# An encoder layer on one core: the embedding gate from eight block products to seven, with its weight sums made during the mixers

## The chip, the core and the metric

The kernel runs on one core of a Trainium2 chip. A core has five engines that work side by side, each through its own list of instructions in order: TensorE (PE, matrix products into the PSUM banks), VectorE (DVE), ScalarE (ACT), GpSimd (POOL) and SyncE (SP), which here issues most of the DMAs. An instruction waits for semaphores of what it needs, and everything behind it on the same engine waits too. The metric is the device time of one execution in microseconds. Of the kernel before, three runs were timed; one further execution was recorded by the hardware profiler.

## The reference

One post-norm encoder layer on 1024 tokens of width 1024, in float32:

```python
u      = x @ W_in                       # 4 x 512 retention, 512 + 128 + 128 attention
group R: bidirectional retention, 8 heads, chunks of 128
group A: windowed attention, 8 query heads on 2 key heads, window 128, sink logit, ALiBi
mix    = concat(R, A) @ W_out
h      = LN1(alpha * x + mix)
ffn    = (silu(h @ W_gate) * (h @ W_up)) @ W_down          # hidden width 2816
ple    = sigmoid(h @ W_pg) * (p @ W_pe)                    # the embedding gate, 1024 x 1024
out    = LN2(alpha * h + ffn + ple)
```

The change concerns `ple`, above all its product `h @ W_pg`, and two places in the mixers.

## The kernel before

Each float32 product is made of three passes: an operand x is split into hi (ScalarE's copy, rounded) and lo = x − hi (VectorE's subtraction; `split`, L77 to L79), and TensorE adds hi·hi, hi·lo and lo·hi in one PSUM bank (`mm3` L81 to L84, and `mm3c` L274 to L278 where several products go into one bank). So a block product of four k tiles by four token tiles is 48 matmuls of 128x512.

The program runs in this order. First the projections `x @ W_in`, 0 to 165 us, with results kept or spilled to DRAM (`ud`). Then the mixers, four pairs i = 0 to 3 (165 to 405 us): each step list (L747 to L760) mixes turns, score products, softmax and values of the retention and the attention, and at every `F` some matmuls of further projections are taken from a queue (`take`, L419), so that TensorE has work between. Only TensorE's order is written out there; a scheduler places the other four engines' instructions. A *turn* is a transpose on TensorE into a PSUM bank, followed by a copy or a split. PSUM has eight banks, two of each of the tags mm, s, t and o; in the mixers, the projections use mm, and turns and the retention's `kv` use t. In pair 0, `first_keys` (L404) and `conv_q` (L385) build the split queries and keys, by ScalarE copies and VectorE operations on 64 partitions x 1024 elements. GpSimd makes the decay tables `sq` and `dt` (L498, L499), which `pt` (L549) needs, and small copies into `sc` (L625) for the scores.

W_out and the first norm follow (405 to 499 us); `to_hT` (L824) turns a token tile of h and splits it into the four blocks `HB[i, j]` (i: half of the features, j: half of the tokens), and scales the tile for the residual.

The embedding gate (499 to 595 us) is four calls of `ple` (L895): output half h by token half, eight k tiles each, 8 x 4 x 3 = 96 matmuls. Its weights come through `load_pg` (L889). Behind each call ScalarE takes the sigmoid (L912), GpSimd multiplies with the embedding piece `ed` (L913; `p @ W_pe` was made in the mixers) and VectorE adds to the residual tile (L914). Beside the calls, as `side`, go the last four `to_hT` and the token sums `t_sums`, from which the FFN's products take their operands. The residual tiles are then stored to `zd` in DRAM (L973, L976) and read back near the end (`load_acc`, L1195).

The FFN (from 595 us) makes gate and up by a scheme of seven block products in place of eight: token halves and feature halves give 2 x 2 blocks, sums of token blocks (TT) meet sums of weight blocks (`s_sums`, on GpSimd), and the seven products are combined. `ahead` (L1376) issues loads and splits a few units ahead. From the first FFN unit on (L1404) all five engines stand in program order.

Of the kernel before, what the change touches and what calls it, by code (L numbers as in the profile page):

```python
# [40 lines left out]
def layer(tc, xT, xn, w_first, w_mt, w_out, w_pg, w_pe, pT, w_gu, w_dn,  # L41
# [343 lines left out]
    def conv_q(i, raw):  # L385

        qs = [bt([P, S], "aq", 3, F32R) for _ in range(2)]
        for g in range(2):
# [4 lines left out]
            dve.scalar_tensor_tensor(qs[g][z, :], raw[a, :], sc_, qs[g][a, :].bitcast(F32), ALU.mult, ALU.subtract)
        return qs
# [7 lines left out]
    def first_keys():  # L402
        pairs[0][2] = conv_q(0, first[0])
        for g in range(2):  # L404
            a = slice(64 * g, 64 * g + 64)
            z = slice(64 * (1 - g), 64 * (1 - g) + 64)
            act.activation(k1[g][a, :], first[1][a, :], AF.Copy)
            dve.tensor_tensor(kz[g][a, :], first[1][a, :], k1[g][a, :].bitcast(F32), ALU.subtract)
            act.activation(k1[g][z, :], first[1][a, :], AF.Copy)
# [72 lines left out]
    class Retention:  # L482
# [1034 lines left out]
```

## Time and profile before

| | |
|---|---|
| median of 3 runs | 1240.6 us (1239.94 to 1241.23) |
| profiled execution | 1243.8 us, span of its trace 1242.0 us, mean granted TensorE clock 0.991 |
| mixers, 165 to 400 us | TensorE busy 218.04 of 235 |
| first gate matmul / first FFN matmul | 499.12 us / 595.42 us |
| TensorE busy, 530 to 610 us | 72.18 of 80 |
| instructions on PE, DVE, ACT, POOL in the trace | 5947, 1320, 922, 395 |

How to read the rows of the profile shown below. A timeline row has start and duration in us, engine, line of the kernel, operation, out<-in by the program's names, and in brackets the idle time of that engine just before and what ended it. A row of grouped instructions has count, then busy us and mean ns of one, then idle time before and its releasers. A row of waits reads "engine, line waited for: us in total, times, longest". A row by windows gives busy time and count of each engine, then the clock that TensorE was granted, the busy share of the DMA engines and GB/s. A row of DMA issues gives count, size and the median us from issue to landing.

### The profile page before, as it was taken

The page shows a single profiled execution, that of the slowest core. Times are in us where ns is not written, and L with a number is a line of the kernel's source. Part 1 is how long each engine was busy: PE and PEld are TensorE (multiplying, and loading weights), DVE is VectorE, ACT ScalarE, POOL GpSimd, SP SyncE. Part 2 cuts the span into 40 slices and gives each one's busy share as a digit, 9 for nine tenths or more (in the row PEclk, how much of TensorE's full clock was granted, in tenths as well). Part 3 has the DMA queues.
Part 4 walks back from the last instruction along what each step waited for, and adds up shares of the span by engine and source line. Part 5 has one row for each costly group of instructions (what it writes and reads, how often), then busy time and mean ns, then how long its engine had stood idle before and what let it go on. Part 6 is the DMA issues. An engine that isn't in the chain of part 4 may idle for free.

```text
span 1242.0 us, 16636 instructions
## 1 busy us (share of the span) xinstructions
PE 1203.1 (97%) x5947; PEld 993.0 (80%) x5947; DVE 772.5 (62%) x1320; ACT 496.9 (40%) x922; POOL 447.7 (36%) x395
## 2 busy tenths in 40 slices
PE   9999989999999999999899999999999999999996
PEld 7778868787878888878688888888888888888885
DVE  7954467777675658497455454555445555865667
ACT  5432355565656503433333233333323334553452
POOL 2652011112111011132467466465564523024235
PEclk9999989999999999999999999999999999999998
DMA  5223230242311422124422233312333149999977
GB/s 221 90 102 119 101 121 18 94 130 85 110 61 42 155 75 81 55 67 165 175 81 90 85 127 128 118 72 74 119 128 127 68 138 284 387 272 205 256 179 203
DMA packets 64899, 161.67 MB, mean 130 GB/s; under 512 B 7729, under 2 KB 9905, under 8 KB 64817
## 3 DMA queue, kind: packets, MB, share of 16 engines
q1 hardware_dynamic: 56176, 143.83, 32.9%
q0 software_dynamic: 8640, 16.78, 7.8%
q8 instruction: 47, 0.77, 0.2%
q14 instruction: 36, 0.29, 0.1%
HBM read 115.76 MB, written 39.58 MB: 125 GB/s over the span
## 4 chain that ended last, share of the span: by engine, by line
PE 66%; issue 9%; DMA 9%; DVE 8%; POOL 5%; ACT 2%; DVEq 0%; SPq 0%; POOLq 0%; ACTq 0%
PE bs L278 4%; PE bs L276 4%; PE bs L277 4%; PE bt L277 4%; PE bt L278 4%; PE bt L276 4%; PE bmm L276 3%; PE bmm L277 3%; PE bmm L278 3%; PE bo L276 3%; PE bo L277 3%; PE bo L278 3%; PE bmm L82 3%; PE bmm L83 3%; PE bmm L84 3%
## 5 line engine op out<-in xcount | busy, mean ns | idle before, releaser
L1035 POOL TENSOR_TENSOR ev<-ev 128x512 f32<-128x512 f32 x33 | 55.7, 1687 | 94.0 <-DVE ev L1050 64.5
L79 DVE TENSOR_TENSOR w<-raw,w 128x512 fp32r<-128x512 f32 x69 | 56.1, 824 | 45.6 <-ACT w L78 45.5
L79 DVE TENSOR_TENSOR w<-H,w 128x512 fp32r<-128x512 f32 x44 | 38.2, 868 | 62.0 <-ACT w L78 62.0
L625 POOL COPY sc<-skb 128x1 f32<-128x1 f32 x64 | 16.7, 269 | 154.5 <-PE bt L646 113.8
L1005 POOL TENSOR_TENSOR H<-ln 128x512 f32<-128x512 f32 x22 | 29.3, 1333 | 96.8 <-DMA ln<-in_w_gu 96.8
L1039 POOL TENSOR_TENSOR ev<-ev,ev 128x512 f32<-128x512 f32 x44 | 62.0, 1421 | 2.6
L1033 ACT ACTIVATE ev<-ev 128x512 f32<-128x512 f32 x33 | 20.9, 633 | 104.4 <-DVE ev L1050 104.4
L78 ACT ACTIVATE w<-raw 128x512 fp32r<-128x512 f32 x69 | 42.0, 625 | 47.9 <-DMA raw<-in_w_pg 13.6
L79 DVE TENSOR_TENSOR u<-H,u 128x512 fp32r<-128x512 f32 x47 | 35.4, 753 | 38.7 <-ACT u L78 38.4
L82 PE MATMUL bmm<-H,w 128*128 128x512 f32 x112 | 50.1, 448 | 0.2 <-ACT H L78 0.2
L913 POOL TENSOR_TENSOR sg<-sg,pe 128x512 f32<-128x512 f32 x16 | 25.1, 1585 | 59.0 <-ACT sg L912 55.5
L810 POOL TENSOR_TENSOR stt<-stt,cst 128x1 f32<-128x1 f32 x8 | 11.5, 1449 | 96.1 <-DVE stt L809 96.1
L78 ACT ACTIVATE u<-H 128x512 fp32r<-128x512 f32 x47 | 29.7, 631 | 40.6 <-PE bs L278 10.7
L634 ACT ACTIVATE sc<-sc,st 128x385 f32<-128x385 f32 (+1 forms) x64 | 37.1, 583 | 19.8 <-DVE st L632 19.6
L84 PE MATMUL bmm<-H,w 128*128 128x512 f32 x112 | 44.7, 399 | 0.0
L83 PE MATMUL bmm<-H,w 128*128 128x512 f32 x112 | 44.5, 397 | 0.0
L630 DVE CUSTOM_DVE_ANT_0 sc<-cst,bs,skb 128x384 f32<-128x384 f32 (+1 forms) x64 | 35.0, 574 | 8.1 <-PE bs L629 7.8
L1009 POOL TENSOR_TENSOR H<-raw,H 128x512 f32<-128x512 f32 x22 | 36.9, 1677 | 0.0
L78 ACT ACTIVATE w<-H 128x512 fp32r<-128x512 f32 x44 | 27.4, 623 | 23.0 <-PE bs L278 8.3
L648 ACT ACTIVATE ptr<-bt 128x384 f32<-128x384 f32 (+1 forms) x64 | 26.6, 457 | 24.7 <-PE bt L646 24.5
L79 DVE TENSOR_TENSOR u<-raw,u 128x512 fp32r<-128x512 f32 x30 | 33.4, 1112 | 5.0 <-ACT u L78 5.0
L914 DVE TENSOR_TENSOR acc<-acc,sg 128x512 f32<-128x512 f32 x16 | 19.1, 1219 | 27.3 <-POOL sg L913 27.3
(757 smaller groups left out, 4068.6 us busy)
## 6 DMA issues: line engine op xcount, KB each, us to landing
ad<-ev SPq DMA_DIRECT2D x33, 512.0 KB, 2.9
raw<-in_w_gu SPq DMA_DIRECT2D x22, 512.0 KB, 4.4
ln<-in_w_gu SPq DMA_DIRECT2D x22, 512.0 KB, 3.5
raw<-ad SPq DMA_DIRECT2D x40, 256.0 KB, 5.5
ln<-ad SPq DMA_DIRECT2D x37, 256.0 KB, 6.5
H<-in_w_dn SPq DMA_DIRECT2D x33, 256.0 KB, 7.1
raw<-in_w_mt SPq DMA_DIRECT2D x12, 512.0 KB, 3.6
h0b<-in_w_dn POOLq DMA_DIRECT2D x24, 256.0 KB, 7.3
```

Of the source, the lines that this page charges most:

```text
L78: act.activation(hi, raw, AF.Copy)
L79: dve.tensor_tensor(lo, raw, hi.bitcast(F32), ALU.subtract)
L82: pe.matmul(o, lh, rh, start=start, stop=False)
L83: pe.matmul(o, lh, rl, start=False, stop=False)
L84: pe.matmul(o, ll, rh, start=False, stop=stop)
L276: pe.matmul(o, lh, rh, start=start, stop=False, skip_group_check=True)
L277: pe.matmul(o, lh, rl, start=False, stop=False, skip_group_check=True)
L278: pe.matmul(o, ll, rh, start=False, stop=stop, skip_group_check=True)
L634: act.activation(sc[g][:, :nk + 1], sc[g][:, :nk + 1], AF.Exp, bias=st_[:, 1, j, g:g + 1], accum_out=st_[:, 2, j, g:g + 1])
L1009: pool.tensor_tensor(s[3], a(0, 1), s[0], ALU.subtract)
L1035: pool.tensor_tensor(c[:, 1, :], c[:, 0, :], c[:, 1, :], ALU.mult)
L1039: pool.tensor_tensor(self.ev[dst][:, 0, :], left, right, op)
```

## The change

1. **The embedding gate by seven products.** `h @ W_pg` is now computed by the same scheme as the FFN, on the same token sums: products 3, 7, 1, 6, 2, 5, 4, of 4 k tiles x 4 token tiles x 3 passes = 48 matmuls each, 336 in place of 384. The weight sums for products 5, 7, 6 and 3 (`ws`) are read from DRAM. The lo half of every second weight tile goes to GpSimd. Products 1 and 6 stay in their banks for products 2 and 5, and the results are combined on VectorE (u, v, f), with sigmoids on ScalarE. The multiplication with `ed` (`embed`, `embed_next`) is taken in single pieces: four on GpSimd, twelve on VectorE, of these eight between FFN units; a GpSimd DMA adds each result to `zd` in DRAM. `to_hT` therefore stores its scaled tile to `zd` at once. All four turns beside product 7 use the banks mm and s. The two token halves exchange their places (`tile_of`). All of it stands in program order on all five engines.
2. **Weight sums in the mixers.** `weight_sums`, twice in pair 0 and twice in pair 1, loads four blocks of W_pg, makes four sums on GpSimd and stores them: 16 loads, 16 sums of 128x512 and 16 stores in all.
3. **First keys in halves.** The operations of `conv_q` and `first_keys` run over 512 columns at a time, all of the first half first.
4. **Three banks for turns.** `tbank` gives the mixers' turns and `kv` the tags t, t, mm in rotation.

```diff
+    wsd = {p: dr.tile([2, P, D], F32, name=f"ws{p}") for p in (5, 6, 7, 3)}
...
     def first_keys():
         pairs[0][2] = conv_q(0, first[0])
-        for g in range(2):
...
+        for c in hs:
+            for g in range(2):
...
+                act.activation(k1[g][a, c], first[1][a, c], AF.Copy)
+                dve.tensor_tensor(kz[g][a, c], first[1][a, c], k1[g][a, c].bitcast(F32), ALU.subtract)
+                act.activation(k1[g][z, c], first[1][a, c], AF.Copy)
+
+    def weight_sums(kt):
+        a, b = atile((P, 2, HF)), atile((P, 2, HF))
+        q, c = kt // 2, hs[kt % 2]
+        for t, i in ((b, 1), (a, 0)):
+            for h in range(2):
+                sp.dma_start(t[:, h, :], w_pg[h, 2 * i + q][:, c])
+        a00, a10, a01, a11 = a[:, 0, :], a[:, 1, :], b[:, 0, :], b[:, 1, :]
+        for p, x, y in ((5, a11, a10), (7, a10, None), (6, a00, a11), (3, a01, a00)):
+            pool.tensor_tensor(x, x, a00 if p == 7 else y, ALU.add)
+            sp.dma_start(wsd[p][q][:, c], x)
...
+    def tbank(shape):
+        tr[0] += 1
+        return bank(("t", "t", "mm")[tr[0] % 3], shape)
...
+            wsum = [(weight_sums, 2 * i + j) if i < 2 else (lambda: None,) for j in range(2)]
...
-                sco(3), F, val(0), val(1), F, ...
+                sco(3), F, wsum[0], val(0), val(1), F, ...
-                val(2), val(3), Q(1), F, more[0], ...
+                val(2), val(3), Q(1), wsum[1], F, more[0], ...
...
+    def pg(p, q):
+        src = wsd[p] if p in wsd else wblk(*{1: (0, 0), 2: (0, 1), 4: (1, 1)}[p])
+        if q == 0:
+            pg_tiles(p)
+        r = rawt(2 * HF)
+        sp.dma_start(r, src[q])
+        for j in range(2):
+            t, x = PG[p][2 * q + j], r[:, hs[j]]
+            act.activation(t[:, 0, :], x, AF.Copy)
+            (pool if j else dve).tensor_tensor(t[:, 1, :], x, t[:, 0, :].bitcast(F32), ALU.subtract)
...
+    def less(e, x, i, j, q, y):
+        c = halves[q]
+        e.tensor_tensor(x, hi(i, j, c), y, ALU.subtract)
+        e.tensor_tensor(x, x, lo(i, j, c), ALU.add)
...
+    def prod(p, bs, start, stop, side={}):
+        w, L = PG[p], LEFT[p]()
+        for kt in range(4):
+            for k in range(4):
+                c = slice(k * P, (k + 1) * P)
+                mm3c(bs[k], L[:, 0, kt, c], L[:, 1, kt, c], w[kt][:, 0, :], w[kt][:, 1, :],
+                     start and kt == 0, stop and kt == 3)
+            for f in side.get(kt, ()):
+                f()
...
+    def embed_next():
+        if not embs:
+            return
+        t, h, f, eng = embs.pop(0)
+        if not es_:
+            e_load(t, h)
+        e = es_.pop(0)
+        if embs:
+            e_load(*embs[0][:2])
+        eng.tensor_tensor(f, f, e, ALU.mult)
+        pool.dma_start(zd[t][:, hs[h]], f, accum_op=ALU.add)
...
+        b7 = banks(TO)
+        prod(7, b7, True, True, {0: [lambda: pg(1, 0), lambda: to_hT(4, ("mm", "s"))], 1: [lambda: to_hT(5, ("mm", "s"))],
+                                 2: [lambda: pg(1, 1), lambda: to_hT(6, ("mm", "s"))], 3: [lambda: to_hT(7, ("mm", "s"))]})
...
+        def t4s(q):
+            less(pool, x3[q], 1, 1, q, x3[q])
+        b1 = banks(MS)
+        prod(1, b1, True, False, {0: [lambda: pg(6, 0), lambda: t2(0)], 2: [lambda: pg(6, 1), lambda: t2(1)]})
+        for k in range(4):
+            dve.tensor_tensor(u[k], u[k], b1[k], ALU.subtract)
+            dve.tensor_tensor(v[k], v[k], b1[k], ALU.add)
+        by = banks(TO)
+        prod(6, by, True, False, {0: [lambda: pg(2, 0), lambda: t1(0)], 2: [lambda: pg(2, 1), lambda: t1(1)]})
+        f = quad()
+        for k in range(4):
+            dve.tensor_tensor(f[k], u[k], by[k], ALU.add)
+        for q in range(2):
+            t4s(q)
+        prod(2, b1, False, True, nextw(5))
+        for q in range(2):
+            t4(q)
+        g = quad()
+        for k in range(4):
+            act.activation(g[k], b1[k], AF.Sigmoid)
+            embed(4 + k, 0, g[k], pool)
+        prod(5, by, False, True, {0: [lambda: pg(4, 0), embed_next], 1: [embed_next], 2: [lambda: pg(4, 1), embed_next],
+                                  3: [embed_next]})
...
+        b4 = banks(MS)
+        prod(4, b4, True, True, {0: [embed_next], 1: [embed_next], 2: [embed_next], 3: [embed_next]})
...
     with tc.manual_schedule(engines={ET.PE, ET.DVE, ET.Activation, ET.Pool, ET.SP}):
+        ple()
...
         ahead(2, 4)
         for k in range(NG):
             gunits[k][1]()
             gunits[k][2]()
+            embed_next()
```

How the instructions now stand is seen at three places. The first is GpSimd's list at the end of the embedding gate. Before, it holds the multiplications with `ed` (pe) and the first weight sums of the FFN (L1005, L1006):

```order
L913 TENSOR_TENSOR sg_5073<-sg_5073,pe_5071 128x512
L913 TENSOR_TENSOR sg_5079<-sg_5079,pe_5077 128x512
L1005 TENSOR_TENSOR H_5232<-ln_5237 128x512
L1006 TENSOR_TENSOR H_5232<-H_5232,raw_5235 128x512
L913 TENSOR_TENSOR sg_5085<-sg_5085,pe_5083 128x512
L913 TENSOR_TENSOR sg_5091<-sg_5091,pe_5089 128x512
```

Now (line numbers of the changed kernel; L930 is the lo half of a weight tile, here of products 5 and 4; L942 and L943 the token sum for product 4; L988 a multiplication with `ed`, L989 the DMA that adds to `zd`):

```order
L942 TENSOR_TENSOR A_4658<-h0b_4645,A_4658 128x1024
L943 TENSOR_TENSOR A_4658<-A_4658,h0b_4645 128x1024
L942 TENSOR_TENSOR A_4659<-h0b_4645,A_4659 128x1024
L943 TENSOR_TENSOR A_4659<-A_4659,h0b_4645 128x1024
L930 TENSOR_TENSOR u_5076<-raw_5079,u_5076 128x512
L930 TENSOR_TENSOR u_5078<-raw_5109,u_5078 128x512
L930 TENSOR_TENSOR w_5151<-raw_5154,w_5151 128x512
L988 TENSOR_TENSOR A_5132<-A_5132,pe_5160 128x512
L989 DMA zd<-A_5132 128x512
L988 TENSOR_TENSOR A_5132<-A_5132,pe_5162 128x512
L989 DMA zd<-A_5132 128x512
L930 TENSOR_TENSOR w_5153<-raw_5194,w_5153 128x512
```

The four token sums stand ahead of product 5's weight tiles, and the multiplications and DMAs between the two halves of product 4's.

The second place is SP's list of DMAs just ahead of the FFN. Before:

```order
L910 DMA pe_5204<-ed 128x512
L910 DMA pe_5210<-ed 128x512
L997 DMA ln_5246<-in_w_gu 128x1024
L997 DMA raw_5391<-in_w_gu 128x1024
L910 DMA pe_5216<-ed 128x512
L910 DMA pe_5222<-ed 128x512
```

Now:

```order
L973 DMA pe_5160<-ed 128x512
L973 DMA pe_5162<-ed 128x512
L973 DMA pe_5178<-ed 128x512
L926 DMA raw_5194<-in_w_pg 128x1024
L973 DMA pe_5200<-ed 128x512
L973 DMA pe_5250<-ed 128x512
L973 DMA pe_5252<-ed 128x512
L973 DMA pe_5268<-ed 128x512
L973 DMA pe_5284<-ed 128x512
L973 DMA pe_5300<-ed 128x512
L1088 DMA raw_5313<-in_w_gu 128x1024
L1088 DMA ln_5315<-in_w_gu 128x1024
```

Nine pieces of `ed`, in two buffers, now stand ahead of the FFN's first weights, where before loads of both kinds alternated.

The third place is GpSimd's list in the first mixer pair, at the decay tables. Before:

```order
L498 TENSOR_TENSOR sq_1292<-sq_1292,masks 128x256
L499 TENSOR_TENSOR dt_1291<-sq_1292 128x128
L498 TENSOR_TENSOR sq_1297<-sq_1297,masks 128x256
L499 TENSOR_TENSOR dt_1291<-sq_1297 128x128
L625 COPY sc_1485<-skb 128x1
```

Now (L423 is a weight sum):

```order
L423 TENSOR_TENSOR A_1578<-A_1578,A_1577 128x512
L423 TENSOR_TENSOR A_1577<-A_1577 128x512
L519 TENSOR_TENSOR sq_1296<-sq_1296,masks 128x256
L423 TENSOR_TENSOR A_1577<-A_1577,A_1578 128x512
L520 TENSOR_TENSOR dt_1295<-sq_1296 128x128
L423 TENSOR_TENSOR A_1578<-A_1578,A_1577 128x512
L519 TENSOR_TENSOR sq_1301<-sq_1301,masks 128x256
L520 TENSOR_TENSOR dt_1295<-sq_1301 128x128
L646 COPY sc_1499<-skb 128x1
```

The first four weight sums stand among the table operations; the other twelve stand in groups of four ahead of copies into `sc`.

More of the change, by code (lines that the diff above doesn't have):

```diff
@@ L403, in first_keys @@
         pairs[0][2] = conv_q(0, first[0])
[L404 to L409, printed above, removed]
+        for c in hs:
+            for g in range(2):
+                a = slice(64 * g, 64 * g + 64)
+                z = slice(64 * (1 - g), 64 * (1 - g) + 64)
+                act.activation(k1[g][a, c], first[1][a, c], AF.Copy)
[11 more added lines that the diff above has]
+            sp.dma_start(wsd[p][q][:, c], x)
     queue = []
@@ L503, in keys @@
             i = self.i
-            tb = bank("t", (P, 2, P))
+            tb = tbank((P, 2, P))
             for j in range(2):
@@ L841, in layer @@
         if kt % 2 == 0:
-            wbig = ct([P, 2, 2, 2, HF], ("h2", "h3")[kt // 2], dt=F32R)
+            wbig = ct([P, 2, 2, 2, HF], ("h0a", "h0b")[kt // 2], dt=F32R)
         r = rawt(2 * HF)
@@ new lines, in layer, with pg_tiles @@
+    PG, nprod = {}, [0]
+    def pg_tiles(p):
+        k = nprod[0]
+        nprod[0] += 1
+        PG[p] = [wp.tile([P, 2, HF], F32R, tag="w", bufs=4, name=nm("w")) if k % 2 == 0 else ct([P, 2, HF], "u", 4, F32R)
+                 for _ in range(4)]
+    def pg(p, q):
[8 more added lines that the diff above has]
+            (pool if j else dve).tensor_tensor(t[:, 1, :], x, t[:, 0, :].bitcast(F32), ALU.subtract)
@@ new lines, in layer, with put @@
+    TT = {}
+    hi = lambda i, j, c: HB[i, j][:, 0, c, :].bitcast(F32)
+    lo = lambda i, j, c: HB[i, j][:, 1, c, :].bitcast(F32)
+    halves = [slice(2 * q, 2 * q + 2) for q in range(2)]
+    def put(n, x, q):
+        split(x, TT[n][:, 0, halves[q], :], TT[n][:, 1, halves[q], :])
+    def less(e, x, i, j, q, y):
+        c = halves[q]
+        e.tensor_tensor(x, hi(i, j, c), y, ALU.subtract)
+        e.tensor_tensor(x, x, lo(i, j, c), ALU.add)
+    MS, TO = ("mm", "mm", "s", "s"), ("t", "t", "o", "o")
@@ new lines, in banks, with quad, nextw, e_load @@
+    def banks(tags):
+        return [bank(t) for t in tags]
+    def quad():
+        ts = [atile((P, 2, HF)) for _ in range(2)]
+        return [ts[k // 2][:, k % 2, :] for k in range(4)]
+    def nextw(p):
+        return {0: [lambda: pg(p, 0)], 2: [lambda: pg(p, 1)]}
+    es_, embs = [], []
+    def e_load(t, h):
+        e = ct([P, HF], "pe", 2)
+        sp.dma_start(e, ed[t][:, hs[h]])
+        es_.append(e)
+    def embed(t, h, f, eng):
+        embs.append((t, h, f, eng))
+    def embed_next():
[9 more added lines that the diff above has]
+        pool.dma_start(zd[t][:, hs[h]], f, accum_op=ALU.add)
@@ L1272, in third @@
             pool.dma_start(x, ln2[1], accum_op=ALU.add)
-        return first, second, third, lambda: sp.dma_start(out[t], x)
+        return first, second, third, lambda: sp.dma_start(out[tile_of(t)], x)
     def tail(products):
```

160 lines of the change are left out of this document (70 added, 90 removed).

## The prediction

> **What bounds the kernel now.** I read the page first: its span, the busy shares, the chain that ended last.
>
> ```profile
> span 1242.0 us, 16636 instructions
> PE 1203.1 (97%) x5947; PEld 993.0 (80%) x5947; DVE 772.5 (62%) x1320; ACT 496.9 (40%) x922; POOL 447.7 (36%) x395
> PE 66%; issue 9%; DMA 9%; DVE 8%; POOL 5%; ACT 2%; DVEq 0%; SPq 0%; POOLq 0%; ACTq 0%
> ```
>
> TensorE sets the time: busy for 97% of the span, and two thirds of the chain. A matmul taken away is worth its issue interval, and another engine matters only where TensorE waits for it. Next, busy time by stage: mixers (165 to 400), most of the embedding gate and the FFN's first units (530 to 610), a stretch from inside the FFN, and the FFN with the down projection.
>
> ```profile
> core 0: us, PE busy (x) PEld busy (x) DVE busy (x) ACT busy (x) POOL busy (x), PEclk, DMA share, GB/s
> 165.00:400.00 235.00, 218.04 (x1610) 182.06 (x1610) 171.32 (x489) 139.79 (x327) 40.90 (x84) 0.99 0.24 81
> 530.00:610.00 80.00, 72.18 (x304) 58.81 (x303) 55.51 (x55) 25.15 (x37) 30.33 (x21) 0.96 0.38 132
> 700.00:800.00 100.00, 100.00 (x443) 82.84 (x442) 54.39 (x68) 31.98 (x54) 58.88 (x40) 1.00 0.27 98
> 610.00:1200.00 590.00, 590.00 (x2605) 488.67 (x2604) 334.44 (x462) 213.61 (x367) 283.22 (x213) 1.00 0.51 157
> ```
>
> From 610 to 1200 TensorE never waits, so neither other token halves nor eight more VectorE multiplies among the gate/up units touch the time there. What can change lies in the mixers (17 us idle) and from 530 to 610 (8 us). In 700 to 800, 443 matmuls of 128x512 take 100 us: 0.2257 us each.
>
> In the gate stage the waits of TensorE, and the rows that bound it, are:
>
> ```profile
> PE bmm L276 <- ACT ev L1056: 4.9, 1, 4.9
> PE bmm L83 <- DVE w L79: 2.9, 1, 2.9
> PE bt L82 <- DVE h L833: 0.4, 1, 0.4
> ...
> 499.12 0.39 PE L82 MATMUL bmm<-w,h0a 128*128 128x512 f32 x1
> ...
> 595.42 0.39 PE L276 MATMUL bmm<-h0a,w 128*128 128x512 f32 x1
> ...
> L831 PE MATMUL bt<-cst,acc 128*128 128x128 f32 x16 | 2.4, 272 | 0.0
> ```
>
> ```profile
> 555.00:560.00 5.00, 2.06 (x6) 1.35 (x5) 4.40 (x6) 0.00 (x0) 1.78 (x2) 0.85 0.39 111
> 560.00:565.00 5.00, 5.00 (x19) 4.03 (x18) 5.00 (x6) 2.15 (x3) 0.00 (x0) 0.81 0.56 203
> 605.00:610.00 5.00, 4.09 (x11) 3.23 (x12) 2.48 (x4) 4.18 (x7) 2.51 (x2) 0.66 0.92 366
> ```
>
> The gate runs from 499.12 to the first FFN matmul at 595.42: 96.3 us. Its 384 matmuls make 86.7 and its 32 turns (two groups of 16, 2.4 busy each) 4.8; 4.8 are lost: 0.4 + 2.9 of waits and about 1.4 of clock (granted 0.85 and 0.81; 19 matmuls in the 5 us from 560, where 22 fit at full clock, and three lost before). Just behind, at 606, comes a wait of 4.9, and 1.6 more by the clock (11 matmuls in 4.09 busy us, where 18 fit). **11.3 us are lost in or just behind the gate.**
>
> The Trainium skill (TensorE: Matmul & The Clock Gate, Part 1) lowers the clock after an idle window of about 3.4 us, for about as long. The trace differs: the 2.9 us wait, below that window, already cost 1.4. By the page, waits below 3.4 us keep full clock, and a short wait of my sum would be 1.4 cheaper. I price every wait near 3 us or more with its clock, from the rows.
>
> **The change part by part.** *Matmuls:* 384 become 336. 48 x 0.2257 = **−10.8**. The turns stay.
>
> *The gate's old waits* go with the old order (**−11.3**); the new order brings its own. I follow it from 499.1 at 0.2257 a matmul: a product of 48 is 10.8. Prod 3 ends at 510; prod 7 with the turns and a bank wait of 0.9 (the 0.4 above, twice) at 526.5; prods 1, 6, 2 at 537, 548, 559. Their weights and sums should be ready: each prod's weight tiles come free during the prod before the last, some 11 us ahead, for a load and two pairs of splits. Half of the sums of T3 now goes to GpSimd, four of 2.5, while TensorE is in prod 3; prod 7 needs them 15 us after they can start. The `zd` stores now stand on SP ahead of prod 6's loads and wait for the last turn's scaling at about 526, 11 us before that prod. I put these at nothing; without that cover each costs TensorE what it is late. The durations:
>
> ```profile
> L79 DVE TENSOR_TENSOR w<-raw,w 128x512 fp32r<-128x512 f32 x14 | 9.2, 680 | 1.6 <-ACT w L78 1.6
> ...
> L1008 POOL TENSOR_TENSOR H<-raw,ln 128x512 f32<-128x512 f32 x2 | 2.6, 1291 | 0.0
> ...
> L1009 POOL TENSOR_TENSOR H<-raw,H 128x512 f32<-128x512 f32 x22 | 36.9, 1677 | 0.0
> ...
> L1271 POOL TENSOR_TENSOR acc<-acc,u 128x1024 f32<-128x1024 f32 x2 | 5.1, 2535 | 0.0
> ...
> 523.93 1.76 DVE L914 TENSOR_TENSOR acc<-acc,sg 128x512 f32<-128x512 f32 x1 [3.98 <-POOL sg L913]
> ...
> 526.81 0.68 DVE L914 TENSOR_TENSOR acc<-acc,sg 128x512 f32<-128x512 f32 x1
> ```
>
> The last two rows show the same VectorE add at 0.68 alone and at 1.76 with a GpSimd multiply beside it: they take turns. GpSimd's own add of 128x512 is 1.29 alone and 1.68 on the mean of the stretches where VectorE works beside it. The Trainium skill (GPSIMD Engine Reference, Key points) has this contention for VectorE instructions with two SBUF inputs; the rows agree. Without it the sum below would be some 2 us lower.
>
> *Prod 5 will wait.* Ahead of its GpSimd weight splits stand four sums t4s of 128x1024 (L942, L943). They need VectorE's t1 of the same half, behind the eight adds on prod 1's banks, so I start them at about 550. At 2.54 each they take 10.1, in turns with VectorE's splits rather 12: 562. Two splits of 1.29 to 1.68 follow, to about 565. Prod 5 starts at 559 and wants the first at 561.7 (12 matmuls on). I take 3.5 of wait (ends 0 and 5) and 1.4 of clock: **+4.9**; prod 5 ends at 574.7, prod 4 at 585.6.
>
> *The FFN's first weights will be late.* Two buffers take the `ed` pieces; each load waits until the piece two before it is multiplied, and on SP the ninth stands ahead of the first w_gu load (L1088). The prices:
>
> ```profile
> raw<-in_w_gu SPq DMA_DIRECT2D x22, 512.0 KB, 4.4
> ...
> pe<-ed SPq DMA_DIRECT2D x16, 256.0 KB, 2.8
> raw<-in_w_pg SPq DMA_DIRECT2D x8, 512.0 KB, 3.4
> ```
>
> From 565 prod 4's first weights land (3.4) near 569 and are split to 571; the first multiply is done at 572.5, the third piece lands at 575.3, the second weight half at 576.3 and is split to 579. Third and fourth multiplies and their DMAs are through at 582.4. The pieces behind them are loaded and multiplied in pairs (2.8 + 0.68 each, VectorE): the seventh is done by 587.3, when the ninth can load and the w_gu load behind it can go; 4.4 later, at 592, the weights are there, and 0.6 for the first split brings 593. TensorE is done at 585.6: 7.4 of wait (ends 2 and 10) and 1.6 of clock: **+9.0**. Behind the late load stand on SP the other w_gu loads, on ACT the first unit's splits (after f's sigmoids) and on GpSimd, after the accumulating DMAs of the first four VectorE pieces, the weight sums for the unit that waited 4.9 before. They have the 24 matmuls of the first units, 5.4 us, for two sums of 1.29; I count no second wait.
>
> *GpSimd's accumulating DMAs* into `zd` (L989) have no equal in this stage before. Elsewhere:
>
> ```profile
> L1155 POOL DMA_DIRECT2D h0b<-in_w_dn x24 | 21.6, 914 | 29.4 <-issue 18.8 <-DVE h0a L79 3.5 <-DVE h L79 2.7
> L1308 POOL DMA_DIRECT2D acc<-R x12 | 11.2, 929 | 26.3 <-issue 17.1 <-DVE R L1305 8.7 <-DVE H L79 0.4
> ```
>
> Each holds GpSimd 0.9, counted above, and then 0.8 (18.8 over 24) to 1.4 (17.1 over 12) of unexplained issue time. Three stand in the chain to the FFN: 2.3 by the first row, 4.3 by the second. Both accumulate 256 KB, like the new ones, but into SBUF; neither is nearer, so I take **+3.3**, the middle, with 0 and 8.4 (below) as ends.
>
> Gate: −10.8 − 11.3 + 0.9 + 4.9 + 9.0 + 3.3 = **−4.0** (ends −20 and +5, from those of the terms).
>
> *Mixers.* The places that the edits meet:
>
> ```profile
> PE bt L456 <- DVE kv L525: 4.7, 1, 4.7
> PE bt L507 <- DVE kv L525: 2.4, 2, 1.2
> PE bt L646 <- ACT ptr L648: 2.0, 3, 0.8
> PE bs L628 <- DVE pt L549: 2.0, 3, 0.7
> PE bt L646 <- ACT rv L457: 1.7, 3, 0.8
> PE bt L521 <- DVE kdec L510: 1.4, 2, 0.9
> ...
> 171.75 0.69 DVE L549 TENSOR_TENSOR pt<-bs,dt 128x512 f32<-128x512 f32 x1 [0.96 <-POOL dt L499]
> 172.48 2.47 DVE L393 SCALAR_TENSOR_TENSOR aq<-A,aq 64x1024 fp32r<-64x1024 f32 x2
> 174.98 1.22 DVE L408 TENSOR_TENSOR kz<-A,k 64x1024 fp32r<-64x1024 f32 x1
> ```
>
> The 4.7 wait is VectorE's: `kv` stands behind two `aq` and a `kz` (3.7 us). Halves let `kv` in earlier but cost two more fixed parts, and the next turn of the same bank then meets the rest: **−2.0** (0 to −4). The other waits on bank t above sum to 7.5; turns on three banks instead of two should hide two fifths: **−3.0** (0 to −6). The third turn shares bank mm with the projections: **+1.0**. The sixteen weight sums are new on GpSimd, 1.29 alone and 1.68 in turns, 21 to 27 us of an engine that is busy 41 of 235. Its idle time covers most; the first sums stand in front of `dt`, for which `pt` already waits 0.96: **+1.3**, one sum. In turns they slow VectorE by up to 16 x 1.08 = 17 us, little of it on TensorE's path: **+1.2**. The 16 loads and 16 stores go past SP; TensorE's waits name no DMA there, so nothing is added. Mixers: **−1.5** (−6 to +5).
>
> Sum: −5.5. The profiled execution took 1243.8 around a span of 1242.0, 3.2 over the median 1240.6; I apply the difference to the median: **1235**.
>
> **Rivals.** *All late weights hidden.* If the t4s are done by 559 and the chain of `ed` loads ends before prod 4 does, 4.9, 9.0 and 3.3 go: 1235.1 − 17.2 = **1218**, its near misses up to 1226. For it: ten of my estimated microseconds hang on starts I placed by hand. Against it: two buffers and SP's order.
>
> *Saving eaten by the chain.* The last stage shows accumulating DMAs at 1212.25, 1214.40, 1218.99 and 1222.71, with work between. If three of the new ones space the chain by 3.7 instead of 0.9 each, 8.4 instead of 3.3: **1240**, no change.
>
> ```profile
> 1212.25 0.91 POOL L1272 DMA_DIRECT2D acc<-u  x1
> ...
> 1218.99 0.90 POOL L1272 DMA_DIRECT2D acc<-u  x1 [0.41 <-POOL acc L1271]
> ...
> 1222.71 0.88 POOL L1272 DMA_DIRECT2D acc<-u  x1 [0.41 <-POOL acc L1271]
> ```
>
> *Slower, in the mixers.* Four sums in a row, 6.7 us in turns, stand ahead of `dt` in the first pair and ahead of the copies `sc` three more times. If the first group is fully exposed (5.4 beyond what I counted) and each other by one sum (5.0 in all): 1235.1 + 10.4 = **1245**. It decides from 5.5 us of further exposed sums on. For it: TensorE waits 2.0 for `pt` already. Against it: GpSimd's copies wait for others, not others for them.
>
> *The mixer edits don't do what they say:* halves and third bank save nothing, the sums cost as counted: 1235.1 + 5.0 = **1240**.
>
> **How the numbers follow.** Chances: forecast 0.48, all hidden 0.18, eaten 0.13, slower 0.14, mixer edits idle 0.07. About 0.2% (2.5 us) is what a measurement of this kernel can tell from none. The forecast (own range 1229 to 1240) gives 0.43 faster, 0.05 the same; all hidden 0.18 faster; eaten 0.02, 0.08, 0.03; slower 0.01 the same, 0.13 slower; edits idle 0.02 and 0.05. Sums: faster 0.65, the same 0.19, slower 0.16. Range 1220 to 1244: 0.08 of the hidden case falls below, 0.12 of the slower one above.
>
> **What would show it.** Right: TensorE 10.8 less busy in the gate; a wait of 2 to 5 us in prod 5 for a GpSimd split behind L943; a wait of 5 to 13 ahead of the first FFN matmul, ended by a w_gu split, with the clock down behind it, and that matmul at about 596; the wait for `kv` at 178 gone or split in two. Wrong: TensorE unbroken from prod 3 into the FFN (the first rival), gaps of over 2 us between the L989 transfers (the second), or `pt` and the scores waiting for `dt` and `sc` behind L423 (the third).

## The result, and the profile after

The changed kernel takes 1271.01 us (median of 4 runs, 1268.75 to 1273.47) against 1240.91 of the kernel before on the same chip: **ratio 1.0242, 95% interval 1.0221 to 1.0264, 30 us slower.** The prediction was 1235, range 1220 to 1244.

The page of the changed kernel (busy times, then the chain that ended last):

```profile
span 1270.5 us, 16734 instructions
PE 1200.0 (94%) x5899; PEld 988.1 (78%) x5899; DVE 797.3 (63%) x1339; ACT 509.5 (40%) x954; POOL 505.0 (40%) x436
PE 78%; DVE 9%; DMA 6%; ACT 3%; issue 3%; POOL 2%; SPq 0%; DVEq 0%; ACTq 0%; POOLq 0%
```

TensorE has its 48 matmuls less, but is busy only 3 us less: the others take longer at a lower clock (granted 0.980 on the mean, 0.991 before), which fell after waits (last section). The waits of TensorE from 495 to 700 us in the changed kernel (line waited for: us in total, times, longest):

```profile
PE bmm L277 <- ACT w L79: 11.8, 1, 11.8
PE bs L277 <- DVE ev L1141: 11.4, 2, 11.0
PE bt L277 <- DVE A L1042: 5.2, 1, 5.2
PE bt L278 <- DVE u L930: 2.6, 1, 2.6
PE bs L277 <- DVE acc L822: 2.5, 1, 2.5
PE bmm L277 <- DVE h0a L855: 2.3, 2, 1.3
PE bt L277 <- ACT H L79: 1.4, 1, 1.4
```

Before, the same stretch had 4.9, 2.9 and 0.4. Four instructions of TensorE's timeline mark the stages (first of W_out, first of the gate, last of the gate, first of the FFN):

```profile
412.70 0.39 PE L83 MATMUL bmm<-w,H 128*128 128x512 f32 x1
...
503.92 0.39 PE L277 MATMUL bmm<-w,h 128*128 128x512 f32 x1
...
606.27 0.39 PE L279 MATMUL bs<-w,h 128*128 128x512 f32 x1
618.48 0.80 PE L277 MATMUL bmm<-h0a,w 128*128 128x512 f32 x1 [11.82 <-ACT w L79]
```

| stretch | before | after | difference |
|---|---|---|---|
| start to the first W_out matmul (projections, mixers) | 407.92 | 412.70 | +4.8 |
| W_out and first norm | 91.20 | 91.22 | 0 |
| embedding gate, to the start of that wait (618.48 − 11.82) | 96.30 | 102.74 | +6.4 |
| wait ahead of the first FFN matmul | 0 | 11.82 | +11.8 |
| first FFN matmul to the end of the span | 646.58 | 652.02 | +5.4 |

The gate's 336 matmuls and turns are 80.6 us of work; of the rest, 14.8 go to waits and 7.4, what is left, to the clock. The last line holds a second new wait of 11.0 us, less the 4.9 that was there before and the clock of both. So the mixers came out at +4.8 where I had −1.5, and the gate with what follows it at +23.6 where I had −4.0.

### The profile page after: what moved, and what is told of

The parts are those of the page before. It is cut to its first block, busy times and chain, and to the rows that moved or that the text cites. A ratio compares the mean times of both kernels' runs of the same rounds, so it can differ in the third digit from the quotient of the medians.

```text
span 1270.5 us, 16734 instructions
## 1 busy us (share of the span) xinstructions
PE 1200.0 (94%) x5899; PEld 988.1 (78%) x5899; DVE 797.3 (63%) x1339; ACT 509.5 (40%) x954; POOL 505.0 (40%) x436
## 4 chain that ended last, share of the span: by engine, by line
PE 78%; DVE 9%; DMA 6%; ACT 3%; issue 3%; POOL 2%; SPq 0%; DVEq 0%; ACTq 0%; POOLq 0%
PE bs L279 5%; PE bs L277 5%; PE bo L277 5%; PE bs L278 5%; PE bo L279 5%; PE bo L278 5%; PE bmm L277 5%; PE bmm L278 5%; PE bmm L279 5%; PE bt L279 5%; PE bt L277 5%; PE bt L278 5%; PE bmm L83 3%; PE bmm L84 3%; PE bmm L85 2%
## 5 line engine op out<-in xcount | busy, mean ns | idle before, releaser
L80 DVE TENSOR_TENSOR w<-raw,w 128x512 fp32r<-128x512 f32 x53 | 47.3, 903 | 54.3 <-ACT w L79 54.2
L80 DVE TENSOR_TENSOR w<-H,w 128x512 fp32r<-128x512 f32 x44 | 41.1, 935 | 61.7 <-ACT w L79 61.7
L79 ACT ACTIVATE w<-raw 128x512 fp32r<-128x512 f32 x53 | 32.5, 624 | 43.0 <-DMA raw<-in_w_gu 16.7
L832 POOL TENSOR_TENSOR stt<-stt,cst 128x1 f32<-128x1 f32 x8 | 11.6, 1451 | 76.7 <-DVE stt L831 70.0
L79 ACT ACTIVATE w<-H 128x512 fp32r<-128x512 f32 x44 | 27.4, 622 | 22.1 <-PE bs L279 7.5
L1097 POOL TENSOR_TENSOR H<-H,raw 128x512 f32<-128x512 f32 x22 | 35.1, 1594 | 1.7
L1246 POOL DMA_DIRECT2D h0b<-in_w_dn x24 | 21.3, 900 | 31.6 <-issue 18.4
L1246 POOL DMA_DIRECT2D H<-in_w_dn x11 | 9.6, 872 | 58.3 <-DMA H<-in_w_dn 51.9
```

The source lines that it names most:

```text
L79: act.activation(hi, raw, AF.Copy)
L80: dve.tensor_tensor(lo, raw, hi.bitcast(F32), ALU.subtract)
```

## The experiments

Each ratio is against the kernel before, timed beside it on the same chip; the us beside it are (ratio − 1) x 1241. The intervals are 0.001 to 0.004 either way, 1 to 5 us; the changed kernel stands at +30.0 on this scale.

### The mixer edits, together and apart

The first asks whether the 4.8 us ahead of W_out come from the mixer edits. Edit: on the kernel before, `weight_sums`, the halves and `tbank`, with the gate left as it was.

> The kernel before with the mixer edits alone (weight sums made and stored, but read by nothing; first keys in halves; turns on three banks) and the old embedding gate. If the mixer edits themselves are what makes the first W_out matmul 4.8 us later in the changed kernel (412.70 against 407.92), this run takes 1246 us, 4 to 6 over the kernel before, and its own W_out starts at 412 to 413. If the delay comes from the new gate's program order reaching forward (its weight loads on SP), this run is within 1.5 us of before. My prediction had 1239 (1.5 less than before).

1250.23 us, **1.0059 [1.0039, 1.0079], +7.3**. The mixer edits alone cost, where I had forecast a small gain. The first W_out matmul is at 415.9 here, with the old gate behind it, so the delay is theirs. In the changed kernel and the runs below that keep its mixers and its gate's start, it lies between 412.7 and 415.6: the +4.8 of the table is the low end of a spread of 3 us. Then each by itself; the three edits:

```diff
+            wsum = [(weight_sums, 2 * i + j) if i < 2 else (lambda: None,) for j in range(2)]
...
-        for g in range(2):
+        for c in hs:
+            for g in range(2):
...
-            tb = bank("t", (P, 4, P))
+            tb = tbank((P, 4, P))
```

> The kernel before with the weight sums in the mixers alone (made and stored, read by nothing). The mixer edits together cost some 8 us (1250 against 1242), and the changed kernel loses 7 more when the third bank is taken out, so sums and halves should cost about 14 without that bank. Theory sums (GpSimd's sums stand among the decay tables: the second dt at 176.11 in place of 171.26, and VectorE takes turns with them): 1248 to 1256. Theory halves (the first keys in halves are what costs): 1242 to 1246.

> The kernel before with the first keys in halves alone. Theory sums: within 2 us of before, 1239 to 1243 (my prediction took 2.0 off). Theory halves: 4 to 14 us over it, 1246 to 1256.

> The kernel before with the mixers' turns on three banks alone. If the bank is worth in the old mixers what it is worth in the changed ones (7 us), 1234 to 1237, faster than before. My prediction's terms (3.0 saved, 1.0 lost): 1240. If it only hides what the sums and halves cause: 1241 to 1243.

Sums 1249.13 us, **1.0053 [1.0032, 1.0074], +6.6**; halves 1243.56, **1.0016 [1.0006, 1.0025], +2.0**; banks 1238.54, **0.9977 [0.9966, 0.9988], −2.9**. Together +5.7, which agrees with the +7.3 of the three at once. The halves were to let the wait of 4.7 for `kv` shrink; in the run with the halves alone it is 5.9. The third bank is the one part that gains, and the kernel before with it beats both kernels, if only by 0.2%.

Why do the sums cost this? In the changed kernel they stand between the first pair's decay tables (GpSimd's timeline, and VectorE's wait for the second table):

```profile
168.90 0.68 POOL L519 TENSOR_TENSOR sq<-sq,masks 128x256 f32<-128x256 f32 x1 [5.49 <-ACT sq L518]
169.54 1.72 POOL L423 TENSOR_TENSOR A<-A,A 128x512 f32<-128x512 f32 x1
171.22 0.91 POOL L520 TENSOR_TENSOR dt<-sq 128x128 f32<-128x128 f32 x1
172.09 1.28 POOL L423 TENSOR_TENSOR A<-A,A 128x512 f32<-128x512 f32 x1
173.34 0.66 POOL L519 TENSOR_TENSOR sq<-sq,masks 128x256 f32<-128x256 f32 x1
174.08 0.46 POOL L520 TENSOR_TENSOR dt<-sq 128x128 f32<-128x128 f32 x1
...
174.56 0.69 DVE L570 TENSOR_TENSOR pt<-bs,dt 128x512 f32<-128x512 f32 x1 [1.72 <-POOL dt L520]
```

The second table starts at 174.08, where before `pt` could already follow it at 171.75. So I moved the sums behind the tables:

```diff
-            wsum = [(weight_sums, 2 * i + j) if i < 2 else ...
+            wsum = [(weight_sums, 2 * (i - 1) + j) if i in (1, 2) else ...
```

> The kernel before with the weight sums alone, in pairs 1 and 2 in place of 0 and 1, where GpSimd's list has them behind the pair's decay tables. Theory tables (the sums cost 8 us because they stand between the first pair's sq and dt): 1242 to 1246. Theory turns (sixteen sums slow VectorE wherever they stand): 1247 to 1251.

1247.68 us, **1.0042 [1.0027, 1.0056], +5.2**. My theory of the tables falls: their place accounts for 1.4 of the 6.6 us, which the intervals do not tell from none. With the sums in pairs 0 and 1, TensorE's waits in the mixers (165 to 415 us) add up to 22.1 in place of 16.6, and the largest new ones are for ScalarE's `rv` and `ptr`. What holds these back (turns with VectorE, 16 loads and 16 stores on SP) I did not take apart.

The third bank taken out of the changed kernel:

```diff
-        return bank(("t", "t", "mm")[tr[0] % 3], shape)
+        return bank("t", shape)
```

> The changed kernel with turns and kv on bank t alone, as before. If the third bank costs more than it saves (TensorE waits 7.2 us in the changed mixers for evacuations of bank mm: 3.2 for es, 1.7 and 1.5 and 0.8 for turns put there), this run is 2 to 5 us below the changed kernel's 1271, that is 1266 to 1269. If the third bank saves what I predicted (2 us net), it is 2 us above: 1273.

1278.36 us, **1.0286 [1.0265, 1.0308], +35.5**: 5.5 worse, not better. The waits on bank mm that I had read as its cost are smaller than those on bank t that it removes (with two banks: 6.1 for `kv`, 3.0, 2.3, 2.2 and others).

### The two waits of the FFN

The chain to the first FFN matmul, in the changed kernel, on VectorE, ScalarE and SP:

```profile
607.42 0.69 DVE L988 TENSOR_TENSOR A<-A,pe 128x512 f32<-128x512 f32 x1 [2.86 <-DMA pe<-ed]
610.23 0.69 DVE L988 TENSOR_TENSOR A<-A,pe 128x512 f32<-128x512 f32 x1 [2.12 <-DMA pe<-ed]
611.99 0.69 DVE L988 TENSOR_TENSOR A<-A,pe 128x512 f32<-128x512 f32 x1 [1.07 <-DMA pe<-ed]
612.60 1.28 DVE L1065 TENSOR_TENSOR A<-A,bmm 128x512 f32<-128x512 f32 x2
...
613.31 2.42 ACT L1066 ACTIVATE A<-A 128x512 f32<-128x512 f32 x4 [9.26 <-DVE A L1065]
617.80 0.63 ACT L79 ACTIVATE w<-raw 128x512 fp32r<-128x512 f32 x1 [2.06 <-DMA raw<-in_w_gu]
...
595.01 16.26 SPq L973 DMA_DIRECT2D pe<-ed  x6
611.32 0.43 SPq L1088 DMA_DIRECT2D raw<-in_w_gu  x1
```

VectorE multiplies as the `ed` pieces land, and f's adds (L1065) stand behind; SP issues six `ed` loads over 16 us, and the w_gu load stands behind. First, four buffers for `ed` (the idle tag sg lends two):

```diff
-        e = ct([P, HF], "pe", 2)
+        e = ct([P, HF], ("pe", "sg")[en[0] % 2], 2)
```

> The changed kernel with four buffers for the pieces of ed in place of two, so that a load of ed waits for the multiplication four pieces before it, and SP is freer to issue the w_gu loads behind. Theory SP (the ed loads that wait for buffers hold the FFN's weights on SP): the waits of 11.8 us at 618 and 11.0 us at 659 fall to 4 or less each, and the time to 1250 +/- 4. Theory GpSimd (accumulating DMAs and weight sums on GpSimd keep the FFN waiting): both waits stay above 8, time 1266 to 1271.

1260.08 us, **1.0148 [1.0128, 1.0169], +18.4**: 11.6 off; the waits are 5.7 and 6.4. Neither theory's number: half of each wait stays. Then SP freed altogether:

```diff
-        sp.dma_start(e, ed[t][:, hs[h]])
+        pool.dma_start(e, ed[t][:, hs[h]])
```

> The changed kernel with the loads of ed (two buffers, as in the change) issued by GpSimd in place of SP, so that no ed load stands ahead of a w_gu load; GpSimd waits for the same multiplications anyway. Theory SP (four buffers took the two FFN waits to 5.7 and 6.4 and 11 us off the time, the rest being loads of ed that still held SP): both waits at 2 or less, 1245 to 1251. Theory GpSimd (the rest is the chain of multiplications and accumulating DMAs): one of the waits stays at 4 or more and the time above 1256, since each load now costs GpSimd another 0.9.

1283.15 us, **1.0333 [1.0309, 1.0357], +41.3**: worse by 11. Its timeline shows why (SP, VectorE, ScalarE):

```profile
592.86 0.33 SPq L1088 DMA_DIRECT2D raw<-in_w_gu  x1
...
625.55 0.69 DVE L988 TENSOR_TENSOR A<-A,pe 128x512 f32<-128x512 f32 x1 [5.36 <-DMA pe<-ed]
627.49 0.69 DVE L988 TENSOR_TENSOR A<-A,pe 128x512 f32<-128x512 f32 x1 [1.25 <-DMA pe<-ed]
628.10 1.28 DVE L1065 TENSOR_TENSOR A<-A,bmm 128x512 f32<-128x512 f32 x2
...
628.82 2.42 ACT L1066 ACTIVATE A<-A 128x512 f32<-128x512 f32 x4 [27.49 <-DVE A L1065]
631.14 0.61 ACT L79 ACTIVATE w<-raw 128x512 fp32r<-128x512 f32 x1
```

The w_gu load now goes out at 592.86, and TensorE still waits, for 23.4 us. SP as the sole cause falls. The split of the landed weight stands on ScalarE behind f's sigmoids, these behind f's adds on VectorE, these behind multiplications that wait for `ed`, whose loads on GpSimd are slower still (5.1 us in the median, 4.1 on SP). In the changed kernel the two lists end 2.1 us apart: the sigmoids at 615.7, the load at 617.8. Freeing one shows the other. So the multiplications themselves were moved:

```diff
-        prod(4, b4, True, True, {0: [embed_next], 1: [embed_next], 2: [embed_next], 3: [embed_next]})
+        prod(4, b4, True, True)
...
             embed_next()
+            if k < 4:
+                embed_next()
```

> The changed kernel with the eight multiplications that stood beside and behind prod 4 moved among the FFN units (two for each of the first four units, then one), so that f's adds and sigmoids and the first w_gu loads come before them on VectorE, ScalarE and SP. Theory order: the first FFN wait of 11.8 falls to 3 or less; the second stays, since twelve ed loads in two buffers now stand ahead of the second w_gu loads on SP: 10 to 20 us, time 1262 to 1274. Theory DMA: the first wait stays above 6.

1266.12 us, **1.0196 [1.0157, 1.0236], +24.3**. The first wait is 2.0, the second 11.7 (and 3.1 at another bank): as theory order had it. The DMA engines have a part too. Between 595 and 660 us, by queue and by load, in the changed kernel:

```profile
q1 hardware_dynamic: 3169, 8.09, 37.5%
q0 software_dynamic: 2160, 3.93, 37.0%
...
zd<-A POOLq DMA_DIRECT2D x14, 256.0 KB, 6.5
pe<-ed SPq DMA_DIRECT2D x13, 256.0 KB, 4.1
raw<-in_w_gu SPq DMA_DIRECT2D x4, 512.0 KB, 8.6
ln<-in_w_gu SPq DMA_DIRECT2D x4, 512.0 KB, 10.0
```

```diff
-        pool.dma_start(zd[t][:, hs[h]], f, accum_op=ALU.add)
```

> The changed kernel without the sixteen accumulating DMAs into zd (the gate term is computed and multiplied, but never added to the residual). Theory DMA (between 595 and 660 these DMAs take 37% of the DMA engines' time for 3.9 MB, and w_gu loads land in 8.6 to 10 us in place of 4.3 and 3.6): ed and w_gu loads land in 3 to 5 us, the FFN waits of 11.8 and 11.0 fall to about 7 and 4, time 1255 to 1261. Theory order (two buffers and the places of the ed loads and multiplications in the lists of SP and VectorE are the cause, whatever the DMA engines do): both waits stay at 9 or more, 1267 to 1271.

1261.06 us, **1.0146 [1.0111, 1.0181], +18.1**: 11.9 off. Loads land in 2.8 (`ed`), 5.1 and 5.9 (w_gu), and the waits are 6.2 and 3.1. That is theory DMA's reading, and the order's part is what stays. Of the 5.6 us by which the first wait falls, 2.4 are the landing of the first w_gu load itself (6.5 us from issue before, 4.1 now). The kernel of this run leaves the gate's term out of the sum, and it also takes off GpSimd the 0.9 us that each of these DMAs holds it; I did not separate the two.

The second wait. SP, ScalarE, VectorE and TensorE in the changed kernel:

```profile
614.13 30.78 SPq L973 DMA_DIRECT2D pe<-ed  x7
645.01 0.37 SPq L1088 DMA_DIRECT2D raw<-in_w_gu  x1
...
652.45 0.63 ACT L79 ACTIVATE w<-raw 128x512 fp32r<-128x512 f32 x1 [14.65 <-DMA raw<-in_w_gu]
656.46 0.63 ACT L79 ACTIVATE u<-raw 128x512 fp32r<-128x512 f32 x1 [3.38 <-DMA raw<-in_w_gu]
657.12 1.10 DVE L80 TENSOR_TENSOR u<-raw,u 128x512 fp32r<-128x512 f32 x1 [2.72 <-ACT u L79]
658.15 0.68 DVE L1141 TENSOR_TENSOR ev<-ev,bs 128x512 f32<-128x512 f32 x1
658.97 0.77 PE L277 MATMUL bs<-h,w 128*128 128x512 f32 x1 [11.01 <-DVE ev L1141]
```

Seven `ed` loads stand on SP ahead of the second set of w_gu loads. The split that waits for one of these is made ahead of its use (the look-ahead is up to eight units), but the evacuation L1141, which frees TensorE's next bank, stands behind it. With a shallower look-ahead:

```diff
-            ahead(2, k + 1 + min(8, 4 + k))
+            ahead(2, k + 1 + min(8, 3 + k // 3))
```

> The changed kernel with a shallower look-ahead in the FFN: after unit k, splits are issued for min(8, 3 + k//3) units ahead in place of min(8, 4 + k), so that the splits of the second set of w_gu weights come on ScalarE and VectorE behind the evacuations of some three more units. Theory look-ahead (at 653 to 658 VectorE holds L1141, which frees bank s, behind a split that waits for a w_gu load): the wait of 11.0 falls to 3 or less, the first wait of 11.8 stays, time 1257 to 1262. Rival (the load itself is late for its own matmuls, by SP and the busy DMA engines): a wait of 8 or more stays, 1267 to 1272.

1264.95 us, **1.0180 [1.0156, 1.0204], +22.3**: 7.7 off; the second wait is 2.5, the first 12.9. Theory look-ahead holds for the waits; the time stays 3 us above the range I gave it.

### Inside the gate

Prod 5's wait, with the t4s (the token sums for product 4) on VectorE, and then with them on GpSimd behind prod 5's splits:

```diff
-            less(pool, x3[q], 1, 1, q, x3[q])
+            less(dve, x3[q], 1, 1, q, x3[q])
```

> The changed kernel with the four sums t4s of 128x1024 on VectorE in place of GpSimd. Theory turns (GpSimd's 2.84 to 3.34 us sums slow VectorE's L942 and L943 from 1.23 to 3.3 and 3.4, and the splits for prod 5 wait behind them): the waits at prod 5 (5.15 and 2.55 us, and their clock) fall by 5 to 8, time 1263 to 1266. Rival (VectorE's list is what is long, not the turns): 4 x 1.23 us more on VectorE keep the waits as they are or up to 3 longer, 1270 to 1274. In both the FFN's waits stay.

```diff
-        for q in range(2):
-            t4s(q)
         prod(2, b1, False, True, nextw(5))
+        for q in range(2):
+            t4s(q)
```

> The changed kernel with the four GpSimd sums t4s behind prod 5's weight splits in place of ahead of them. Theory turns (the sums slow VectorE's L942 and L943 to 3.4 and 3.3 us and so hold the adds that free bank t, and they hold prod 5's splits on GpSimd): the waits of 5.15 and 2.55 us at prod 5 fall to 1 or less with their clock loss, 1259 to 1264. Rival (prod 5's late operands come from late loads on SP, since raw<-ws stood 6.8 us at 562): the waits stay above 4 together, 1268 to 1272.

On VectorE 1274.15 us, **1.0257 [1.0235, 1.0279], +31.9**: prod 5 waits 6.6 in one piece, the rival's case. Put late 1278.14 us, **1.0285 [1.0252, 1.0318], +35.4**: prod 5's waits do fall to 1.8, but prod 4 waits 4.8 for its weights, behind T4's splits on ScalarE, and the FFN 17.7. The local reading was right and the time went the other way.

The stores of `zd` put behind prod 7:

```diff
-        sp.dma_start(zd[t], accs[t])
+        if t < 4:
+            sp.dma_start(zd[t], accs[t])
```

> The changed kernel with the zd stores of tiles 4 to 7 behind the whole of prod 7 on SP, in place of inside its turns. If the stores hold the loads of prod 1's and prod 6's weights on SP (raw<-in_w_pg issued at 528.69 behind two stores, ScalarE waiting 4.5 for it with two turns behind), the waits at 535, 537 and 549 (1.30, 0.96, 1.39, 0.53) fall to 1 in sum, and the time by 3 to 5: 1266 to 1268. If they only move the hold to prod 6's loads: 1270 to 1273.

1273.49 us, **1.0249 [1.0216, 1.0282], +30.9**. Prod 1's waits fall from 2.3 to 0.3, prod 6's 1.4 and 0.5 stay, and the first FFN wait is 13.6 in place of 11.8: what is won ahead of the last chain seems to be waited for at its end. That is not shown by this run alone, since the run with the shallower look-ahead, whose gate is the changed kernel's, has 12.9 there.

### All holds undone at once

Beside the edits shown above for the buffers, the look-ahead, the multiplications, the stores and the place of the weight sums, and with the first keys no longer in halves:

```diff
-        prod(1, ..., {0: [lambda: pg(6, 0), lambda: t2(0)], ...
+        prod(1, ..., {0: [lambda: pg(6, 0), lambda: t2(0), lambda: t1s(0), lambda: t4s(0)], ...
...
+        fin = ple()
         ahead(2, 4)
+        fin()
```

> The changed kernel with every hold found so far undone at once: four buffers for ed; f's adds and sigmoids behind the first FFN splits; the twelve VectorE multiplications among the FFN units (two for each of the first three units); the shallower look-ahead; the zd stores of tiles 4 to 7 behind prod 7; the sums for T4 and T1 in prod 1 in place of prod 6 and 2; keys not in halves; weight sums in pairs 1 and 2. Theory order: the FFN's two waits fall to 3 in sum (20 us and 3 of clock), prod 5's to 2 (6 and 3), prods 1 and 6 save 3, the mixers 5: 1271 - 38 = 1233, between 1228 and 1240. Rival (each list in program order only hands the wait on to the next one, as when the t4s were put later): 1246 or more.

1244.92 us, **1.0019 [0.9998, 1.0041], +2.4**: 27.7 off, not to be told from before, and 12 above my 1233, nearly at the rival's 1246. What is left of TensorE's waits from 495 to 700:

```profile
PE bt L277 <- ACT H L79: 6.2, 2, 4.9
PE bmm L277 <- DVE ev L1148: 2.8, 2, 1.6
PE bmm L277 <- DVE A L1070: 1.6, 1, 1.6
```

The FFN's waits are gone but for 1.6 and two short ones; one of 4.9 has come up in prod 6, for the second half of T2, whose VectorE sums now stand behind T1's and take turns with the t4s. The last two runs ask after it, and after the sums' price here:

```diff
-        ... lambda: t1s(0), lambda: t4s(0)], ...
+        ... lambda: t1s(0)], ...
+        for q in range(2):
+            t4s(q)
```

```diff
-            wsum = [(weight_sums, 2 * (i - 1) + j) if i in (1, 2) else ...
+            wsum = [(lambda: None,)] * 2
...
-        src = wsd[p] if p in wsd else wblk(...)
+        src = wblk(*{1: (0, 0), 2: (0, 1), 4: (1, 1), 5: (1, 0), 7: (0, 0), 6: (1, 1), 3: (0, 1)}[p])
```

> The kernel of the run before (all holds undone) with the GpSimd sums t4s back behind prod 6, while VectorE's sums for T1 stay in prod 1. There TensorE waited 4.88 us in prod 6 for T1's split, whose sums took turns with the t4s. Theory turns: that wait falls to 1 or less with 1.4 of clock, prod 5 stays below 2, 1245 - 6 = 1239. Rival (handed on): prod 5 or 4 takes it over, 1243 to 1246.

> The same kernel without the weight sums in the mixers: no loads, sums or stores there, and prods 5, 7, 6 and 3 read plain blocks of W_pg, so that the gate's values are not the layer's; the gate's own work is unchanged. It shows the price of the sums. If they cost here what they cost in the kernel before (5 to 8 us), 5 to 8 below the run beside it: 1231 to 1234. If the third bank hides them, within 2 of it.

With the t4s back behind prod 6: 1243.34 us, **1.0011 [0.9995, 1.0028], +1.4**. That wait in prod 6 is down to 0.7 and 0.5, and prod 2 has one of 5.8 for a VectorE split that stands behind T1's sums and eight adds: handed on, the rival's case. Without the weight sums: 1235.08 us, **0.9934 [0.9913, 0.9955], −8.2**, so the sums cost 9.6 here, give or take 3; the first W_out matmul is at 404.65 in place of 414.45, so they lie ahead of the gate. That this run stands at my 1235 is luck: the kernel is not the one that I predicted. It pays nothing for the sums, has the old keys and most of the waits undone, and its gate reads plain blocks of W_pg, so that the values are not the layer's. What it shows is that a seven-product gate beats the old one once its sums are free and its order is worked over: by 8.2 us, of which the third bank may be 2.9.

## Why the prediction was wrong

*Matmuls, −10.8.* Right: 5899 in place of 5947. The saving was there and was overspent.

*"From 610 to 1200 TensorE never waits, so neither other token halves nor eight more VectorE multiplies touch the time there", and "I count no second wait".* This is the step that failed worst. That TensorE does not wait there before says that the lists of the other engines were in time, not that they had room for late entries. The multiplications among the FFN units put seven `ed` loads on SP ahead of the second set of w_gu loads; the late load holds a split, and the split holds an evacuation. It measured 11.0 plus clock; the shallower look-ahead alone took 7.7 off.

*The FFN's first weights, +9.0 and +3.3.* The chain was the right one, mis-sized: 11.8 of wait. It started at 582.4 rather than 565, since everything ahead of it was late, and I priced its loads by the medians of a kernel without accumulating DMAs (2.8 and 4.4; measured 4.1 and 8.6). I named f's sigmoids ahead of the split, but gave that list no time; moving the loads to GpSimd showed that VectorE's and ScalarE's lists end about as late. And I looked for the accumulating DMAs' price in GpSimd's spacing (0.8 to 1.4 each), where GpSimd's rows show 0.3 ahead of those behind its own multiplications; the runs put much of it on the DMA engines instead: without these DMAs the loads land sooner, and the time falls by 11.9 us.

*Prod 5, +4.9.* The place and the cause (the t4s in turns with VectorE: put late, they leave a wait of 1.8) were right, the size was not: 5.2 and 2.6 plus clock. What came late was VectorE's add, which frees the bank, and VectorE's split, not GpSimd's.

*"Their weights and sums should be ready ... I put these at nothing".* Wrong: prods 3, 1 and 6 wait 2.5, 2.3 and 1.9, for T3's sums and norm work on VectorE, for turns behind a late weight on ScalarE, and for T2. The first is 0.5 in four of the nine runs whose code is the same from the mixers to there, so 2 us of it come and go. Each is under 3 us, and I had priced only the large ones; with prod 5's wait and the clock they ate the saving.

*Mixers, −1.5.* The third bank was right (−2.0 against −2.9 measured). The halves had the wrong sign (−2.0 against +2.0). The sums were priced 2.5 and cost 6.6. The slower rival named their place; at 1245 it had a seventh of the loss, and its mechanism, the place ahead of the tables, is not what the runs bear out.

*The form of the sum.* I added stalls along TensorE as if each list were otherwise idle. The runs with the t4s put late and with T1's sums early show that these waits are not additive: the engines' lists feed each other in order, and a wait undone comes up at the next entry. With the holds undone together, 27.7 of the 30 us are gone.

VectorE's turns with GpSimd cost more than I priced: GpSimd's four t4s took 12.7 us where I had 12, but VectorE's two sums beside them took 6.7, where alone they take 2.5, and I had nothing for that. The contention that the Trainium skill (GPSIMD Engine Reference, Key points) names for VectorE instructions with two SBUF inputs is confirmed by these rows (last section). The clock rule of the Trainium skill (TensorE: Matmul & The Clock Gate, Part 1), which I quoted with an idle window of about 3.4 us, again differs from the trace: behind a wait of 2.52 us the granted clock was 0.75 (last section).

## What to carry to other kernels

When work is put into program order on several engines, price not only its own duration but what stands behind it in each list: a load that waits for a buffer on SP, a split that waits for that load, an evacuation behind the split. A stage in which TensorE never waits is no proof of room; ask for each new entry when its operand lands, and which bank's release stands behind it. Trading matmuls for sums and transfers pays only by what these leave: 10.8 us saved here met 7 to 10 us of weight sums, though GpSimd, which makes them, was busy for only 41 of the mixers' 235 us before.

## What the runs showed of the hardware

*Accumulating DMAs are dear on the DMA engines.* In the rows between 595 and 660, 3.93 MB of them took 37.0% of the sixteen engines' time, as much as 8.09 MB of plain transfers (37.5%): twice the time per byte. The adding seems to cost this more than GpSimd's queue does: where that queue carried the plain `ed` loads as well (between 590 and 660 of that run), 6.82 MB took 47.3% of 70 us, 33 us, where the rate of the adding DMAs alone (24 us for 3.93 MB) would give 42 by my estimate. The w_gu loads beside them landed in 8.6 and 10.0 us; without them, in the same window, in 5.1 and 5.9. I had not looked for this.

*VectorE and GpSimd in turns.* In the changed kernel (VectorE's and GpSimd's timelines):

```profile
561.84 1.22 DVE L942 TENSOR_TENSOR ln<-h,A 128x1024 f32<-128x1024 f32 x1
568.29 3.41 DVE L942 TENSOR_TENSOR ln<-h,A 128x1024 f32<-128x1024 f32 x1
578.26 1.27 DVE L1042 TENSOR_TENSOR A<-A,bt 128x512 f32<-128x512 f32 x2
...
567.78 2.84 POOL L942 TENSOR_TENSOR A<-h0b,A 128x1024 f32<-128x1024 f32 x1
570.70 3.25 POOL L943 TENSOR_TENSOR A<-A,h0b 128x1024 f32<-128x1024 f32 x1
577.34 3.23 POOL L943 TENSOR_TENSOR A<-A,h0b 128x1024 f32<-128x1024 f32 x1
```

The same VectorE sum (of the other half) takes 1.22 alone and 3.41 beside GpSimd's, which take 2.84 and 3.25 where the prediction's row for 128x1024 has 2.54. The adds L1042 at 578.26, with one operand in PSUM, run beside GpSimd's L943 at 0.64 each, not slowed.

*The clock falls after short waits.* Windows of 5 us of the changed kernel, after the wait of 2.52 at 508.64, and after 1.39 and 0.53 at 549:

```profile
510.00:515.00 5.00, 5.00 (x18) 3.99 (x18) 5.00 (x8) 2.14 (x4) 3.10 (x2) 0.75 0.05 20
550.00:555.00 5.00, 4.84 (x15) 3.87 (x15) 4.15 (x4) 0.78 (x1) 1.25 (x1) 0.66 0.34 105
```

The granted clock is 0.75 and 0.66, 18 and 15 matmuls where 22 fit; yet over 535 to 540, with waits of 1.30 and 0.96, it stays 1.00. No run here says which short wait costs and which not.
